# Mixer C of a two-layer encoder: 32 by 32 diagonal blocks gathered by copies of ScalarE instead of masks and sums of VectorE

## The chip, the cores and the metric

The kernel runs on one core of a Trainium2 chip. The metric is the device time of one execution in microseconds (us), the median of the runs shown. The engines are TensorE (PE in the profile; its weight loads are PEld), VectorE (DVE), ScalarE (ACT), GpSimd (POOL) and the queue of SyncE (SP), which issues nearly all transfers. Each engine executes its own instructions in order; semaphores let one wait for another.

## The reference, cut to what matters

The reference is an encoder of two layers over 256 tokens of 1024 channels. In each layer four mixers work on one joint projection of x: A (a gated mLSTM), B (dilated attention), C (a gated delta rule) and D (windowed attention). Their outputs are gated, summed and projected, and a feed-forward part follows: a SwiGLU in layer 0, eight experts in layer 1. Mixer C has 4 heads of 64 channels and runs in two directions over chunks of 64 tokens. For each chunk, head and direction it solves a triangular system of 64 unknowns:

```python
a_strict = jnp.where(strict, jnp.einsum('bhnid,bhnjd->bhnij', k_beta, k) * decay, 0.0)
rhs = jnp.concatenate([v * beta[..., None], k_beta * jnp.exp(gc)[..., None]], axis=-1)
sol = lax.linalg.triangular_solve(a_strict, rhs, left_side=True, lower=True, unit_diagonal=True)
u, w = sol[..., :Dv], sol[..., Dv:]
```

The rest of the mixer is a scan over the chunks with matrix products.

## The kernel before, in words

**The large products.** The weights are 32-bit. Each piece of 128 by 1024 is loaded into `raw` (line 251), ScalarE rounds it into a high half `wh` (line 256), and VectorE, sometimes GpSimd, subtracts to get the low half `wl` (line 259). TensorE multiplies three times (line 162): high by high, high by low, low by high. So each group of products needs one cast of ScalarE and one subtraction of VectorE first. `raw`, `wh` and `wl` live in rings of a few buffers: a cast waits until TensorE has finished with the buffer that it is to write.

**The mixers** are Python generators. `mixing` (line 1151) issues the projections one after the other and after each piece advances the open mixers by some steps, so that their small instructions stand between the large products. The order on each engine is made by a planner when the kernel is built: it takes instructions by priority as their inputs come ready in its own model of time, and a mixer's steps get a priority that is raised by 56 places (`AHEAD`). After that the order is fixed: an instruction that waits holds up all behind it on its engine.

**Mixer C** (`mix_c`, line 745). `systems(t)` makes, for each half t of the tokens (128 each) and direction d, a tile U of 128 partitions by 4 heads by 128 columns, which holds the triangular systems. `leaves(d)` (line 869) inverts the 32 by 32 blocks on U's diagonal, four for each head and half, all at once; `unit(d, t)` (line 911) combines the inverses with TensorE into the full ones (V is the transpose of W, the two tiles of the inverse) and advances the scan.

`leaves` first has to bring the blocks together. The diagonal blocks lie at partitions 32k to 32k+31 and columns 32k to 32k+31 of each head. Line 879 multiplies U by the mask `blk32`, in which partition group k is one for block k only, into a tile `cum`; line 880 sums over k, so that each partition keeps the 32 columns of its own block, and writes them into y at a distance of 32 elements. Line 882 copies the result three more times, and line 883 transposes all 32 by 32 blocks of y into z. Then come 31 steps of forward substitution on VectorE (lines 897 and 898, two instructions of 0.2 to 0.3 us each) that update `cX`, a transpose into `cWc` (line 902), and for each half t line 906 spreads the result back: a product with the same mask writes W, zero outside the diagonal blocks, and line 907 transposes it into V.

After that `unit(d, d)` runs first, then `unit(d, 1 - d)`. In `unit`, the first product (line 924) reads U and W, the second (line 931) reads V. The next direction's solve starts when the first one's `cWc` is written, because `cX` has one buffer. `cW` and `cV` have two buffers each, and `cum` shares a ring of two (`cs`) with the tiles of `systems`. `leaves` runs four times in all, twice a layer.

Of the kernel before, what the change touches and what calls it, by code (L numbers as in the profile page):

```python
# [12 lines left out]
OP = mybir.AluOpType  # L13
AX = mybir.AxisListType
PSUM = bass.MemoryType.PSUM

P = 128
# [102 lines left out]
class Encoder:  # L120
# [624 lines left out]
    def mix_c(self):  # L745
        mp, nc, c = self.mp, self.nc, self.c
# [89 lines left out]
        r3 = lambda x: x[:].rearrange("p (h i) -> p h i", i=P)  # L836
        U, at, V, W = {}, {}, {}, {}
# [31 lines left out]
        def leaves(d):  # L869


            yz = self.m8("cYZ")
            y, z = yz[:, :1024], yz[:, 1024:]
            yv = y.rearrange("p (i x t h) -> p i x t h", x=4, t=2, h=4)
            k32 = c["blk32"][:, None, :, None].to_broadcast([P, 4, 4, 32])
            for t in range(2):
                m = self.t2("cum", "cs")
                mv = m[:].rearrange("p (h k i) -> p h k i", k=4, i=32)
                self.tt(mv, U[d, t].rearrange("p h (k i) -> p h k i", i=32), k32, OP.mult)
                nc.vector.tensor_reduce(yv[:, :, 0, t, :].rearrange("p i h -> p h i"), mv.rearrange("p h k i -> p h i k"), AX.X, OP.add)  # L880
            y4 = y.rearrange("p (i x m) -> p i x m", x=4, m=8)
            nc.vector.tensor_copy(y4[:, :, 1:4], y4[:, :, 0:1].to_broadcast([P, 32, 3, 8]))
            nc.vector.transpose(z, y)
            zv = z.rearrange("p (i j) -> p i j", j=32)
            x = mp.tile([P, 8, 32], F32, name="cX", bufs=1)
            nc.gpsimd.tensor_copy(x[:], c["own32b"].rearrange("p (q r) -> p q r", q=8))
            tmp = mp.tile([P, 8, 32], F32, name="cXt", bufs=1)
            yield
            for n in range(31):
                i = 31 - n if d else n  # L890
                rows = slice(0, i) if d else slice(i + 1, 32)
                cs = slice(i // 4, 8) if d else slice(0, i // 4 + 1)
                sh = [P, cs.stop - cs.start, rows.stop - rows.start]
                f = zv[:, rows, i][:, None].to_broadcast(sh)
                pv = x[:, cs, i:i + 1].to_broadcast(sh)
                tv = tmp[:, cs, rows]
                self.tt(tv, f, pv, OP.mult)
                self.tt(x[:, cs, rows], x[:, cs, rows], tv, OP.subtract)
                if n % 3 == 2:
                    yield  # L900
            wc = mp.tile([P, 256], F32, name="cWc", bufs=1)
            nc.vector.transpose(wc[:], x[:].rearrange("p q r -> p (q r)"))
            wcv = wc[:].rearrange("p (c t h) -> p t h c", t=2, h=4)
            for t in range(2):
                w, vv = self.t2("cW", "cW"), self.t2("cV", "cV")
                self.tt(w[:].rearrange("p (h k c) -> p h k c", k=4, c=32), wcv[:, t][:, :, None, :].to_broadcast([P, 4, 4, 32]), k32, OP.mult)
                nc.vector.transpose(vv[:], w[:])
                W[d, t], V[d, t] = r3(w), r3(vv)
            yield
# [86 lines left out]
        for d in range(2):  # L996
            yield from leaves(d)
            both = [unit(d, t) for t in (d, 1 - d)]
            for _ in range(3):
                for q in both:  # L1000
                    next(q)
                    yield
# [636 lines left out]
```

## Time and profile before

| what | value |
|---|---|
| median of 3 runs | 1399.38 us (1396.96 to 1399.58) |
| the profiled execution, its own time | 1402.63 us |
| its span, first to last instruction | 1400.8 us |
| granted TensorE clock, mean over the span | 0.979 of full speed |
| TensorE busy | 1331.2 us (95%) |
| VectorE busy | 1074.6 us (77%) |
| ScalarE busy | 744.2 us (53%) |
| GpSimd busy | 146.2 us (10%) |

Busy is the time in which an engine executes instructions; matmuls are pipelined and their ends are modelled, so a busy TensorE is not one at its peak. The page also cuts the span into 40 slices of 35 us. `leaves` runs in slices 3 to 6 (layer 0, about 102 to 190 us) and 20 to 22 (layer 1, about 680 to 766 us):

```profile
PE   7999999999999999999989999997999999999995
DVE  6879876775885655678888478568988888888887
ACT  5535453454364443344434446434777778677673
PEclk9999999999999999999999999998999999999997
```

Each digit is the busy share of one slice in tenths (9 is 90% or more), counted from slice 0 at the left. PEclk is the clock granted to TensorE in tenths of full speed.

### The profile page before, as it was taken

Reading aid. Unit: us, or ns where it says so; the run is one execution under the profiler, and the core shown is the slowest. Engines: PE = TensorE matmul, PEld = TensorE weight load, DVE = VectorE, ACT = ScalarE, POOL = GpSimd, SP = SyncE. Lnnn points to the kernel's source line nnn. Section 1 sums busy time; section 2 is a strip of 40 time slices with the busy share of each in tenths; the row PEclk is TensorE's granted clock in tenths of the full one; section 3 lists DMA queues with packets and bytes.
Section 4 is the critical chain, followed back from the end, with each engine's and each line's share of the span. In section 5 each row is a group of like instructions: output and inputs, shape, how many; then the busy total and the mean of one; then the engine's idle time right before and its main releaser. Section 6 shows DMA issues by size and latency. Waiting matters only on the chain. (4 is left out here: it accounts for less than half of the span.)

```text
span 1400.8 us, 23007 instructions
## 1 busy us (share of the span) xinstructions
PE 1331.2 (95%) x8699; PEld 1151.7 (82%) x8702; DVE 1074.6 (77%) x1869; ACT 744.2 (53%) x1097; POOL 146.2 (10%) x119
## 2 busy tenths in 40 slices
PE   7999999999999999999989999997999999999995
PEld 7877879989889998888678889986778878877873
DVE  6879876775885655678888478568988888888887
ACT  5535453454364443344434446434777778677673
POOL 1000200022200000100120001220211110211110
PEclk9999999999999999999999999998999999999997
DMA  7532512485596553234152237745989899989982
GB/s 248 172 106 65 157 61 77 151 304 183 174 299 185 193 187 100 96 103 127 59 161 91 76 104 266 245 127 184 350 301 377 307 328 325 359 309 353 354 307 76
DMA packets 155750, 281.90 MB, mean 201 GB/s; under 512 B 11120, under 2 KB 58480, under 8 KB 155632
## 3 DMA queue, kind: packets, MB, share of 16 engines
q1 hardware_dynamic: 153136, 273.54, 57.9%
q10 hardware_dynamic: 1152, 4.19, 0.9%
q0 software_dynamic: 1344, 2.62, 0.5%
q8 instruction: 70, 1.15, 0.3%
q14 instruction: 48, 0.39, 0.1%
HBM read 276.65 MB, written 2.10 MB: 199 GB/s over the span
## 5 line engine op out<-in xcount | busy, mean ns | idle before, releaser
L259 DVE TENSOR_TENSOR wl<-raw,wh 128x1024 fp32r<-128x1024 f32 (+3 forms) x515 | 612.9, 1217 | 155.3 <-ACT wh L256 139.9
L256 ACT CAST wh<-raw 128x1024 fp32r<-128x1024 f32 (+3 forms) x539 | 525.1, 1006 | 311.5 <-PE mm L162 244.3
L162 PE MATMUL mm<-wh,xh 128*128 128x512 f32 (+4 forms) x736 | 192.0, 370 | 3.8 <-ACT wh L256 2.5
L162 PE MATMUL mm<-wh,xl 128*128 128x512 f32 (+4 forms) x736 | 184.3, 365 | 0.0
L162 PE MATMUL mm<-wl,xh 128*128 128x512 f32 (+4 forms) x544 | 149.9, 368 | 8.5 <-DVE wl L259 8.5
L162 PE MATMUL mm<-xh,wh 128*128 128x256 f32 x960 | 142.3, 287 | 13.2 <-ACT wh L256 7.3
L162 PEld LDWEIGHTS mm<-wh,xh 128*128 128x128 f32 x736 | 129.8, 190 | 26.9 <-ACT wh L256 4.8
L162 PEld LDWEIGHTS mm<-wh,xl 128*128 128x128 f32 x736 | 130.7, 190 | 19.9 <-issue 0.7
L162 PE MATMUL mm<-xl,wh 128*128 128x256 f32 x960 | 141.2, 287 | 0.0
L162 PE MATMUL mm<-xh,wl 128*128 128x256 f32 x960 | 138.2, 282 | 0.0
L162 PEld LDWEIGHTS mm<-xh,wh 128*128 128x128 f32 x960 | 125.4, 192 | 15.5 <-ACT wh L256 7.3
L162 PEld LDWEIGHTS mm<-xl,wh 128*128 128x128 f32 x960 | 126.0, 193 | 1.1 <-issue 0.3
L162 PEld LDWEIGHTS mm<-xh,wl 128*128 128x128 f32 x960 | 123.2, 189 | 0.8 <-issue 0.2
L162 PEld LDWEIGHTS mm<-wl,xh 128*128 128x128 f32 x544 | 94.7, 191 | 25.8 <-DVE wl L259 10.8
L259 POOL TENSOR_TENSOR wl<-raw,wh 128x1024 fp32r<-128x1024 f32 (+1 forms) x24 | 62.0, 2585 | 343.5 <-ACT wh L256 250.9
L1056 POOL TENSOR_TENSOR mg<-mg,th 128x512 f32<-128x512 f32 x24 | 44.5, 1883 | 360.2 <-DVE th L142 360.2
L162 PE MATMUL mm<-wh,hth 128*128 128x512 f32 x176 | 56.6, 397 | 0.0
L162 PE MATMUL mm<-wl,xl 128*128 128x512 f32 (+1 forms) x192 | 56.6, 376 | 0.0
L162 PE MATMUL mm<-wl,hth 128*128 128x512 f32 x176 | 55.7, 395 | 0.0
L162 PE MATMUL mm<-wh,htl 128*128 128x512 f32 x176 | 55.6, 394 | 0.0
L162 PE MATMUL mm<-yT,wh 128*128 128x256 f32 x320 | 43.2, 284 | 0.0
L162 PEld LDWEIGHTS mm<-wl,xl 128*128 128x128 f32 x192 | 35.7, 188 | 6.1 <-DVE wl L259 0.5
(371 smaller groups left out, 1713.9 us busy)
## 6 DMA issues: line engine op xcount, KB each, us to landing
raw<-moe_w_in SPq DMA_DIRECT2D x215, 512.0 KB, 6.2
raw<-w_in_in SPq DMA_DIRECT2D x132, 512.0 KB, 4.1
raw<-ffn_w_in SPq DMA_DIRECT2D x66, 512.0 KB, 3.7
raw<-moe_w_in SPq DMA_DIRECT2D x64, 384.0 KB, 4.5
raw<-w_out_in SPq DMA_DIRECT2D x16, 512.0 KB, 3.5
raw<-w_branch_d_in SPq DMA_DIRECT2D x8, 512.0 KB, 4.8
raw<-w_in_in SPq DMA_DIRECT2D x8, 396.0 KB, 3.6
raw<-w_branch_b_in SPq DMA_DIRECT2D x4, 512.0 KB, 3.3
```

The costliest lines, as they stand in the source:

```text
L162: return self.nc.tensor.matmul(o, l, r, start=start, stop=stop, skip_group_check=True)
L256: self.nc.scalar.copy(h[:, :m * n], raw[:, :m * n])
L259: eng.tensor_sub(l[:, :m * n], raw[:, :m * n], h[:, :m * n])
L1056: self.nc.gpsimd.tensor_tensor(m, m, x, OP.add)
```

## The change

Line 879 and 880 (masks and sums) become eight copies of ScalarE in each `leaves`: for each half t and each block k, the 32 partitions of the block by 4 heads by 32 columns go from U straight to their place in y. The copy that repeats the result three times moves from VectorE to ScalarE. At the end, line 906 (the product with the mask) becomes a memset of W by GpSimd and four copies of ScalarE, one for each block. The transposes stay on VectorE. The tile `cum` is no longer used, and the last loop takes the halves in the order d, 1 - d instead of 0, 1.

```diff
-            k32 = c["blk32"][:, None, :, None].to_broadcast([P, 4, 4, 32])
+            parts = [slice(32 * k, 32 * k + 32) for k in range(4)]
             for t in range(2):
-                m = self.t2("cum", "cs")
-                mv = m[:].rearrange("p (h k i) -> p h k i", k=4, i=32)
-                self.tt(mv, U[d, t].rearrange("p h (k i) -> p h k i", i=32), k32, OP.mult)
-                nc.vector.tensor_reduce(yv[:, :, 0, t, :].rearrange("p i h -> p h i"), mv.rearrange("p h k i -> p h i k"), AX.X, OP.add)
+                for r in parts:
+                    nc.scalar.copy(yv[r, :, 0, t, :].rearrange("p i h -> p h i"), U[d, t][r, :, r])
             y4 = y.rearrange("p (i x m) -> p i x m", x=4, m=8)
-            nc.vector.tensor_copy(y4[:, :, 1:4], y4[:, :, 0:1].to_broadcast([P, 32, 3, 8]))
+            nc.scalar.copy(y4[:, :, 1:4], y4[:, :, 0:1].to_broadcast([P, 32, 3, 8]))
             nc.vector.transpose(z, y)
...
-            for t in range(2):
+            for t in (d, 1 - d):
                 w, vv = self.t2("cW", "cW"), self.t2("cV", "cV")
-                self.tt(w[:].rearrange("p (h k c) -> p h k c", k=4, c=32), wcv[:, t][:, :, None, :].to_broadcast([P, 4, 4, 32]), k32, OP.mult)
+                nc.gpsimd.memset(w[:], 0.0)
+                for r in parts:
+                    nc.scalar.copy(r3(w)[r, :, r], wcv[r, t])
                 nc.vector.transpose(vv[:], w[:])
                 W[d, t], V[d, t] = r3(w), r3(vv)
```

## Rows read from the trace of the kernel before

**Rows 1.** The page's busy times: us (share of the span) xinstructions, whole span.

```profile
PE 1331.2 (95%) x8699; PEld 1151.7 (82%) x8702; DVE 1074.6 (77%) x1869; ACT 744.2 (53%) x1097; POOL 146.2 (10%) x119
```

**Rows 2.** Waits of PE, 684:730 and 148:153: us in total, times, longest us.

```profile
PE mm L162 <- DVE wl L259: 3.7, 1, 3.7
...
PE mx L162 <- DVE cW L134: 1.2, 1, 1.2
```

**Rows 3.** Timeline 723:726: start us, us, engine, line, op, out<-in, xcount [idle before <-releaser].

```profile
723.47 0.45 DVE L902 STREAM_TRANSPOSE cWc<-cX 128x256 f32<-128x256 f32 x1
...
724.15 2.21 DVE L134 TENSOR_TENSOR cW<-cWc,c 128x512 f32<-128x512 f32 x2
...
725.40 0.46 PE L162 MATMUL mx<-cW,cU 32*32 32x32 f32 x16 [1.88 <-DVE cW L134]
```

**Rows 4.** Tile view of cW, under "who waited for it (us, times)".

```profile
  PE mx L162: 3.6, 3
```

**Rows 5.** Timeline of PE, 697:708.

```profile
697.79 0.64 PE L162 MATMUL mm<-wh,xl 128*128 128x256 f32 x4
702.15 1.22 PE L162 MATMUL mm<-wl,xh 128*128 128x512 f32 x4 [3.72 <-DVE wl L259]
```

**Rows 6.** Timeline of ACT, 685:800.

```profile
693.72 1.05 ACT L256 CAST wh<-raw 128x1024 fp32r<-128x1024 f32 x1 [1.20 <-PE mm L162]
...
697.87 0.79 ACT L145 ACTIVATE bk<-mx 128x128 f32<-128x128 f32 x4 [2.43 <-PE mx L166]
707.26 0.59 ACT L508 COPY bvn<-mm 128x512 f32<-128x512 f32 x1 [8.60 <-PE mm L162]
```

**Rows 7.** Timeline of DVE, 680:702.

```profile
680.56 1.12 DVE L142 SCALAR_TENSOR_TENSOR cU<-mx,cbeta,cdec 128x128 f32<-128x128 f32 x4 [1.31 <-ACT cdec L145]
...
693.71 0.68 DVE L134 TENSOR_TENSOR cum<-cU,c 128x512 f32<-128x512 f32 x1
...
695.27 1.10 DVE L880 TENSOR_REDUCE cYZ<-cum 128x128 f32<-128x512 f32 x1
...
699.63 1.23 DVE L883 STREAM_TRANSPOSE cYZ<-cYZ 128x1024 f32<-128x1024 f32 x1
...
700.88 1.21 DVE L259 TENSOR_TENSOR wl<-raw,wh 128x1024 fp32r<-128x1024 f32 x1
```

**Rows 8.** Groups by form, DVE, whole span: xcount | busy us, mean ns | idle before.

```profile
L134 DVE TENSOR_TENSOR cW<-cWc,c 128x512 f32<-128x512 f32 x8 | 8.8, 1139 | 0.1
L880 DVE TENSOR_REDUCE cYZ<-cum 128x128 f32<-128x512 f32 x8 | 8.6, 1075 | 0.0
L134 DVE TENSOR_TENSOR cum<-cU,c 128x512 f32<-128x512 f32 x8 | 5.5, 684 | 0.0
...
L882 DVE COPY cYZ<-cYZ 128x768 f32<-128x768 f32 x4 | 2.2, 552 | 0.0
```

**Rows 9.** Windows: stretch, us, busy us of each engine, PEclk (granted clock), DMA share, GB/s.

```profile
703.00:707.00 4.00, 4.00 (x12) 3.14 (x11) 3.73 (x12) 0.00 (x0) 0.00 (x0) 0.57 0.88 253
727.00:731.00 4.00, 4.00 (x49) 3.71 (x48) 3.65 (x9) 2.62 (x4) 2.04 (x4) 0.57 0.41 129
148.00:152.00 4.00, 2.66 (x32) 2.40 (x33) 3.79 (x10) 1.53 (x5) 2.55 (x4) 1.00 0.73 218
```

**Rows 10.** Groups by form, ACT, whole span.

```profile
L256 ACT CAST wh<-raw 128x768 fp32r<-128x768 f32 x64 | 51.1, 838 | 10.7 <-PE mm L162 10.6
...
L208 ACT CAST yT<-yb 128x256 fp32r<-128x256 f32 x4 | 2.6, 653 | 0.7 <-DVE yb L134 0.7
...
L208 ACT CAST ath<-mm 128x256 fp32r<-128x256 f32 x4 | 1.5, 376 | 0.0
```

**Rows 11.** Groups by form, POOL, whole span.

```profile
L834 POOL MEMSET cS<- 128x256 f32 x4 | 1.2, 323 | 0.0
```

**Rows 12.** Waits of all engines, whole span: us in total, times, longest us.

```profile
ACT wh L256 <- PE mm L162: 244.3, 215, 3.1
```

## The prediction

> **What bounds the kernel now.** I read the page first: TensorE is busy 95% of the span and ScalarE 53% [rows 1], so a change on VectorE and ScalarE can win only what TensorE loses while it waits for them, and only in the two stretches where mixer C runs. I went on from the page to the waits of TensorE in those stretches, to the timeline of each engine around the longest wait, and to the granted clock there.
>
> In layer 1, between 684 and 730 us, TensorE waits 3.7 us once for a low weight half `wl` [rows 2] and 1.9 us once for `cW` [rows 3]. The tile view of `cW` puts all of TensorE's waits for it at 3.6 us in three places [rows 4]: these 1.9, then 1.2 at 150 us in layer 0 [rows 2], and so 0.5 at the third, in layer 1's second direction at 766 us.
>
> The wait for `wl` is the one to look at closely. TensorE ends a group at 698.4 and starts the next at 702.15 [rows 5]. ScalarE had the high half `wh` done at 694.8 [rows 6]; VectorE turned to `wl` only at 700.88 [rows 7]. From 693.71 until then its queue held, among other things, the whole preparation of the second direction of `leaves`: two masks, two sums, the copy and the transpose. In front of this `wl` stand 0.68 + 1.10 + 0.69 + 1.05 + 0.55 = 4.1 us of the very instructions that the change takes from VectorE ([rows 7] show the first of the two pairs, whose second ran at 697.16 and 697.92; the copy's 0.55 is in [rows 8]).
>
> [...] I call 3.7 + 1.7 = 5.4 us gap 1, and 1.9 + 1.7 = 3.6 us gap 2.
>
> **The change part by part.** *Off VectorE.* 8 masks (5.5 us), 8 sums (8.6), 4 copies (2.2) and 8 products into `cW` (8.8) go: 25.1 us in four calls [rows 8], 6.3 a call. The two transposes of the blocks stay. Nearly all of this lies beside TensorE's work; on the path lie the 4.1 us in front of the `wl` of gap 1. With them gone and nothing put in their place, that `wl` starts near 696.8 and is ready at 698.0, before TensorE asks at 698.4. I count gap 1 as gone: -5.4 us. Late next on VectorE would be the solve's steps and the `wl`s behind this one, each of 1.2 us.
>
> *Onto ScalarE.* 64 copies of 32 partitions by 128 elements and 4 copies of 128x768. No row shows a copy of this shape with both operands in SBUF. Below stands the dense one of 128x128 from PSUM, four in 0.79 us [rows 6], 0.20 each: 12.6 us for 64. Above stands a strided one: the split of `yb` into `yT`, which writes every fourth element, takes 0.653 us for 256 elements where a dense one takes 0.376 [rows 10]; 0.277 more for 256 is 0.14 for 128, so 0.34 each and 21.8 us. The 128x768 copy goes by the cast of that shape, 0.84 [rows 10], 3.4 for four. Together 16 to 25 us; I take the strided end, as both copies gather elements that lie apart (512 bytes in U, 32 bytes in `wcv`). [...]
>
> ScalarE is idle from 698.7 to 707.26 in the place of gap 1 [rows 6], and over the run its extra 25 us raise it from 744 to 769 us. The block copies need only U, whose last part was done at 681.7 [rows 7]; so most of them fill its idle time, and I cost them at nothing. Without that cover the price is a `wh` cast that comes up to 2.7 + 0.84 = 3.5 us late behind one call's block copies.
>
> *The wait that is added, at the blocks.* The transpose of the blocks on VectorE now waits for 9 instructions of ScalarE. Behind it in VectorE's order stand solve steps and `wl`s, and for those TensorE waits. At gap 1 that decides: 0 if ScalarE ran the copies in its earlier idle time, all of gap 1 back if they stand behind the `bk` copies, which themselves waited for TensorE until 697.87 [rows 6]: 698.7 + 2.7 + 0.8 + 1.23 (transpose) + 1.21 (`wl`) = 704.6 against 702.1 now. I take 0, because nothing of higher priority needs ScalarE for that long before 697.
>
> *The wait that is added, at W.* TensorE's first product of a unit needs W of the first t. Before: the transpose `cWc` ends at 723.92, `cW` follows, and TensorE starts at 725.40 [rows 3], 1.5 us later. After: four copies by 0.34, 1.36 us, and two hand-overs between engines, for which I add 0.1 each (an estimate from 0.15 us between the end of the first `cW` and TensorE's start): 1.6. By the dense price it would be 1.0. In layer 1 the path stays the same within 0.1. In layer 0, where no `wl` stands between, the 1.14 us of one `cW` [rows 8] and a hand-over, 1.25, become 1.6: +0.3. In the second direction the first unit is t = 1, whose W was the second product and now comes first, 1.1 us sooner: the 0.5 us wait goes. The order of t costs nothing else. ScalarE's queue is held meanwhile, and behind it stand `wh` casts, which are made ahead of use.
>
> *GpSimd.* 8 memsets of 128x512; the one of 128x256 takes 0.32 us [rows 11], so 0.32 to 0.65 each. They need only a free `cW` buffer, which in the first direction is free from the start and in the second from the end of the first direction's solve, a whole solve ahead. I cost them at nothing; a `bv` transfer in front of one in GpSimd's order would be the price, and by 0.65 us for each.
>
> *The sum.* -5.4 (gap 1) + 0.1 (gap 2) + 0.3 (layer 0) - 0.5 (second direction) = -5.5 us against the profiled execution, 1402.6, which makes 1397.1. That execution lay 3.2 us above the median of the three runs, 1399.4; against the median it is 1393.9, say **1394.0**. Its own range, with gap 1 between half and wholly gone and gap 2 shorter by half at best, is 1391 to 1397.
>
> **The rivals.** *All of the gaps close* (-5.4 - 3.6 - 1.2 - 0.5 = -10.7): 1388.7. For it: 8 us of what goes (the block preparation of both calls) stand ahead of the first `cW` of a layer on the same engine. Against it: the order of TensorE is planned with the shorter work too, and its place for W moves up as well.
>
> *The wait only changes its name.* VectorE stands at the transpose of the blocks, waiting for ScalarE, and gap 1 stays (704.6 against 702.1 worked out above, at worst), or the new order, planned anew for every engine, opens another gap of that size: 1399.4, give or take 2. For it: the copies are the lowest in priority when they are issued. Against it: ScalarE's idle time.
>
> *Slower: W behind a held cast.* ScalarE takes its instructions in order. If a `wh` cast stands in front of the W copies, they start late by its wait for TensorE, 244.3 us over 215 waits or 1.1 us on average [rows 12], and its own 1.05: 2.2 us in each of the four places, where TensorE has just shown that it waits for W. In layer 0 the two waits then pass 1.9 us, where the clock fell, 1.7 each: 4 x 2.2 + 2 x 1.7 - 5.4 = +6.8, 1406.2. It decides from 5.4 / 4 = 1.35 us of lateness per place. For it: three of four places already wait for W. Against it: over the run ScalarE is idle 47% of the time [rows 1], and if a cast is held for TensorE, TensorE still has matmuls of its own to run.
>
> **How the numbers follow.** About 0.2% (2.8 us) is what a measurement of this kernel can tell from no change. The forecast 0.45, all gaps closed 0.13, the wait under another name 0.23, slower 0.19. Faster by over 0.2% takes the first two less the part of the first above 1396.6, 0.55; within it, 0.26; slower, 0.19. The range runs from 1388 (all gaps) to 1403 (half of the slower case).
>
> **What would show it.** Right: no wait of TensorE for `wl` over 2 us between 684 and 730 us and a granted clock of 1.00 behind the place; VectorE busy some 25 us less than before, ScalarE near 769 us; 0.3 us or more for a block copy; the waits for `cW` now for ScalarE, still about 1 to 2 us. Wrong: the transpose of `cYZ` with an idle time before it that ScalarE ended; W copies that start more than 1.4 us after `cWc`; new waits of TensorE for `wh` in 90 to 150 or 684 to 770 us; the clock falling at a place where it had held.

## The result, and the profile after

The changed kernel is slower: 1411.34 us median of 20 runs (1399.41 to 1422.79), against 1397.59 for the kernel before in the same job (20 runs, 1393.36 to 1400.47). The ratio is 1.0095, with a 95% interval of 1.0073 to 1.0116. The forecast was 1394.0 us. Ratios and their intervals, here and below, leave out executions more than 1.5% above the fastest of their kernel (2 of these 20, the tail of the loss described below), while medians, clocks and net times are of all executions.

The profiled execution took 1399.5 us, which is the short end of those runs; another profiled execution (e1, below) took 1405.1. The page's busy times, in us, answer to [rows 1]:

```profile
PE 1335.7 (96%) x8699; PEld 1156.4 (83%) x8702; DVE 1055.5 (76%) x1841; ACT 773.6 (55%) x1165; POOL 151.1 (11%) x127
```

The waits of all engines over the span (us in total, times, longest us) answer to [rows 2] and [rows 4]:

```profile
PE mm L162 <- DVE wl L259: 4.8, 5, 1.0
...
PE mx L162 <- ACT cW L906: 2.8, 2, 2.0
...
DVE cYZ L881 <- ACT cYZ L880: 1.1, 1, 1.1
```

The 3.7 us wait for `wl` is gone: none is longer than 1.0. TensorE's waits for `cW` are 2.8 us in all where they were 3.6, the longest 2.0 where it was 1.9. TensorE's idle time, the span less its busy time on the page, fell from 69.6 to 61.9 us. By the waits alone the forecast stands. What does not stand is the clock. The timeline at W in layer 1, the place of [rows 3]:

```profile
711.70 0.44 DVE L900 STREAM_TRANSPOSE cWc<-cX 128x256 f32<-128x256 f32 x1
712.18 3.51 ACT L906 COPY cW<-cWc 32x128 f32<-32x128 f32 x8 [2.06 <-DVE cWc L900]
...
712.65 0.43 PE L162 MATMUL mx<-cW,cU 32*32 32x32 f32 x8 [1.99 <-ACT cW L906]
...
713.97 0.63 PE L162 MATMUL mx<-cW,cU 32*32 32x32 f32 x8
...
715.71 0.85 ACT L256 CAST wh<-raw 128x792 fp32r<-128x792 f32 x1
```

and the windows around it (columns as in [rows 9]; the last three are the granted clock, the DMA share and GB/s):

```profile
698.00:703.00 5.00, 5.00 (x45) 5.00 (x44) 4.62 (x17) 1.56 (x3) 2.17 (x4) 1.00 0.59 163
708.00:713.00 5.00, 2.71 (x24) 2.11 (x22) 3.86 (x15) 2.29 (x8) 1.32 (x3) 1.00 0.42 118
713.00:718.00 5.00, 5.00 (x56) 4.39 (x54) 3.07 (x8) 3.42 (x8) 2.20 (x5) 0.50 0.40 125
723.00:728.00 5.00, 5.00 (x30) 3.90 (x29) 0.52 (x3) 1.21 (x4) 0.79 (x2) 0.50 0.89 321
733.00:738.00 5.00, 5.00 (x29) 4.76 (x29) 1.92 (x9) 2.51 (x6) 0.00 (x0) 0.50 0.00 0
738.00:743.00 5.00, 5.00 (x36) 5.00 (x35) 4.21 (x12) 1.71 (x3) 0.00 (x0) 0.77 0.05 7
743.00:748.00 5.00, 5.00 (x45) 4.41 (x44) 4.05 (x12) 1.19 (x3) 0.00 (x0) 1.00 0.80 216
```

TensorE waits 1.99 us for W, as it waited 1.88 before. Behind that wait the clock lay at 0.50 of full speed from 713 to about 740 us, where before it was back at 1.00 by 731:

```profile
731.00:734.00 3.00, 3.00 (x38) 2.40 (x37) 2.10 (x8) 0.47 (x2) 0.00 (x0) 1.00 0.48 161
```

(this row is of the kernel before). In those 27 us TensorE is recorded as busy all the time, with 29 or 30 products in 5 us (723 and 733 us) against 45 at the full clock (698 and 743 us); VectorE, which waits 8.08 us for one of its products (until 731.67), is busy 0.52 of 5 us in 723 to 728. By the clock, 27 us at 0.50 lose 13.5, an estimate.

The 20 runs show the same as a sum. Their time follows the mean clock of the execution: 1399.5 us at 0.975, 1411 at 0.968, 1419 at 0.960. If an execution of 1400 us loses 1400 x (1 - clock), what is left is an estimate of its time at full clock, called *net* here: 1372 us before and 1364 after. So the changed kernel has 8 us less to do on the path, and pays for it with a mean clock of 0.967 instead of 0.982, 21 us. (Among the 20 runs themselves 0.01 of the clock goes with 12.8 us, where the estimate takes 14; by that slope it is some 5 us less to do and 19 us paid.)

The prices of the new instructions, groups by form of ScalarE and of GpSimd (xcount | busy us, mean ns | idle before):

```profile
L906 ACT COPY cW<-cWc 32x128 f32<-32x128 f32 x32 | 13.7, 429 | 6.5 <-DVE cWc L900 6.0
L878 ACT COPY cYZ<-cU 32x128 f32<-32x128 f32 x32 | 13.3, 416 | 1.2 <-DVE cU L142 0.9
L880 ACT COPY cYZ<-cYZ 128x768 f32<-128x768 f32 x4 | 3.3, 833 | 0.1
```

```profile
L904 POOL MEMSET cW<- 128x512 f32 x8 | 4.1, 528 | 4.7 <-DVE cV L907 2.8 <-PE mx L162 1.8
```

### The profile page after: what moved, and what is told of

It reads as the page before. It is cut to its first block, busy times and chain, and to the rows that moved or that the text cites. A ratio compares the mean times of both kernels' runs of the same rounds, so it can differ in the third digit from the quotient of the medians.

```text
span 1397.6 us, 23081 instructions
## 1 busy us (share of the span) xinstructions
PE 1335.7 (96%) x8699; PEld 1156.4 (83%) x8702; DVE 1055.5 (76%) x1841; ACT 773.6 (55%) x1165; POOL 151.1 (11%) x127
## 5 line engine op out<-in xcount | busy, mean ns | idle before, releaser
L162 PE MATMUL mm<-wh,xl 128*128 128x512 f32 (+4 forms) x736 | 187.5, 369 | 0.0
L162 PE MATMUL mm<-wl,xh 128*128 128x512 f32 (+4 forms) x544 | 153.5, 372 | 4.8 <-DVE wl L259 4.8
L162 PE MATMUL mm<-xh,wh 128*128 128x256 f32 x960 | 139.4, 285 | 9.3 <-ACT wh L256 6.6
L162 PE MATMUL mm<-xl,wh 128*128 128x256 f32 x960 | 138.0, 283 | 0.0
L162 PEld LDWEIGHTS mm<-xl,wh 128*128 128x128 f32 x960 | 123.2, 189 | 1.0 <-issue 0.5
```

The costliest lines, as they stand in the source:

```text
L162: return self.nc.tensor.matmul(o, l, r, start=start, stop=stop, skip_group_check=True)
```

## The experiments

Two theories were set against each other. *Clock*: the loss is TensorE's clock, which falls behind a wait and stays down because few large products stand beside the small ones of the units. *Queue*: ScalarE's copies hold the casts behind them, TensorE waits, and the clock only follows. In the expectations, theory 1 and the theory of the mix are *clock*, theory 2 and the theory of ScalarE are *queue*; those of e2 and e3 say which half of the change each would blame. "Large products" are those of the projections (`mm`, 128x256 to 128x264); they are counted below in TensorE's instruction order from the first product that reads W to the last product of that unit, in the first direction of layer 0 / layer 1. That order is fixed when the kernel is built. The table has all kernels but e1, e5 and e8 (in the text below), each with 6 to 20 executions; "mean clock" is the median over them of the granted clock of a whole execution, and the ratio is to the kernel before in the same job:

| kernel | large products | mean clock | median us | ratio (95%) |
|---|---|---|---|---|
| before (all jobs) | 42/44 | 0.982 | 1396.3 to 1397.7 | 1 |
| the change | 35/35 | 0.967 | 1411.3 | 1.0095 (1.0073 to 1.0116) |
| e2 blocks only | 43/42 | 0.982 | 1392.2 | 0.9962 (0.9938 to 0.9987) |
| e3 W only | 35/43 | 0.976 | 1404.8 | 1.0058 (1.0025 to 1.0092) |
| e4 order of t only | 42/44 | 0.982 | 1396.7 | 1.0011 (0.9990 to 1.0033) |
| e6 W copies on VectorE | 37/45 | 0.979 | 1397.4 | 0.9995 (0.9949 to 1.0041) |
| e7 wider steps | 37/37 | 0.974 | 1399.4 | 0.9996 (0.9956 to 1.0035) |
| e9 fill ahead of W | 35/38 | 0.974 | 1405.1 | 1.0037 (1.0005 to 1.0068) |
| e10 blocks only, fill | 43/38 | 0.981 | 1395.4 | 0.9984 (0.9962 to 1.0006) |
| e11 other order of blocks | 33/39 | 0.967 | 1411.4 | 1.0086 (1.0051 to 1.0121) |
| e12 blocks only, idle copies | 34/42 | 0.973 | 1405.9 | 1.0031 (1.0002 to 1.0059) |
| e13 W of t = 1 later, 300 | 52/62 | 0.976 | 1399.6 | 1.0009 (0.9989 to 1.0029) |
| e14 W of t = 1 later, 250 | 52/34 | 0.974 | 1404.0 | 1.0045 (1.0024 to 1.0065) |
| e15 W copies on GpSimd | 34/41 | 0.974 | 1409.0 | 1.0092 (1.0065 to 1.0119) |
| e16 blocks only, later W | 61/63 | 0.984 | 1386.3 | 0.9930 (0.9905 to 0.9956) |
| e17 before, later W, 300 | 68/45 | 0.983 | 1396.5 | 0.9991 (0.9967 to 1.0015) |
| e18 before, later W, 150 | 34/45 | 0.982 | 1395.6 | 1.0011 (0.9991 to 1.0031) |

**The parts one by one.** e1 is the change once more. e2 has the block copies, with W by the mask on VectorE and the halves in the order 0, 1 (the edit at W):

```diff
-                nc.gpsimd.memset(w[:], 0.0)
-                for r in parts:
-                    nc.scalar.copy(r3(w)[r, :, r], wcv[r, t])
+                self.tt(w[:].rearrange("p (h k c) -> p h k c", k=4, c=32), wcv[:, t][:, :, None, :].to_broadcast([P, 4, 4, 32]), k32, OP.mult)
```

e3 has the new W with the blocks as before, and e4 only the order of t:

```diff
-            for t in range(2):
+            for t in (d, 1 - d):
```

> The changed kernel as it is, for a profile of an ordinary execution (its profiled one was among its shortest, 1399.5 us at a mean granted clock of 0.975; most lay at 1409 to 1420 and 0.968 to 0.96). Theory 1 (clock): TensorE does the same work and waits no longer than in the short execution, and the 10 to 20 us more are stretches of 20 us or more at the lower clock behind the first direction's wait for W, in layer 0, in layer 1 or in both; time and mean clock go together, some 14 us for 0.01. Theory 2 (queue): ScalarE's copies hold up casts, and TensorE's waits for wh or wl add up to 10 us more than before, with the clock a consequence.

> Only the blocks by ScalarE; W by the masked product of VectorE as before, halves in the order 0, 1. Theory 1: what moves the units among other large products is the shorter work of VectorE before the solve, so this kernel has the long stretch at the lower clock too: 1405 to 1415, clock under 0.97. Theory 2 (the W copies do the harm): 1391 to 1396, as the gain without the harm.

> Only W by a memset and ScalarE's copies; blocks by masks and sums as before, halves in the order 0, 1. Theory 1: near the kernel before, 1395 to 1401, clock 0.975 or more, as the solve ends where it did. Theory 2: 1405 to 1415, with the wait for W at 2 us or more in each layer.

> The kernel before with the halves of the last loop in the order d, 1 - d, nothing else. Both theories: within 2 us of before; the wait for W in the second direction of layer 1 (0.5 us) gone. If this one is slower by 5 us or more, the order of t moved the units and neither theory's reason is the cause.

e1 took 1405.1 us at a clock of 0.972, with 0.50 from about 717 to 741 us: the stretch is no accident of one profile. e2 is faster than both kernels, e3 slower, e4 neither. So the block copies give what was forecast for the change, -5.3 us (-8.7 to -1.8), and the harm comes with W. In e3 TensorE waits for W 0.65 us in layer 0 and 1.03 us in layer 1, less than in the kernel before, and the kernel is slower all the same. The parts do not add up: 0.4% won, 0.6% and 0.1% lost make 0.3%, and the change loses 0.95%. Each variant is planned anew, and e3's order in layer 1 keeps 43 large products where the change's has 35. e2's windows at W in layer 1, behind a wait of 2.07 us:

```profile
710.00:715.00 5.00, 2.93 (x35) 2.68 (x35) 4.79 (x12) 1.00 (x3) 3.31 (x5) 0.95 0.67 212
715.00:720.00 5.00, 5.00 (x69) 4.29 (x67) 3.83 (x13) 1.62 (x3) 2.09 (x4) 0.70 0.38 113
720.00:725.00 5.00, 5.00 (x46) 4.03 (x45) 2.65 (x11) 2.38 (x8) 0.04 (x1) 1.00 0.70 222
```

The wait is as long as the changed kernel's, but the clock is back at 1.00 by 720. What differs is TensorE's order behind the wait, here with the number of products of each kind:

```
changed: W 4, large 3, W 4, large 6,  V 5, W 8, V 3, large 5, V 8, large 2, transposes 4, large 6
e2:      W 8, large 15,               V 5, W 8, V 3, large 9, V 8, large 1, transposes 4, large 4
```

**Large products added, small pieces moved.** e5 and e8 put a dense product without use in front of each group of the first direction's units, in the changed kernel and in the kernel before; e6 makes the W copies on VectorE; e7 gives each step of those units one more place in the turn of the mixers:

```diff
+            def bank():
+                o = self.bmx()
+                if d == 0:
+                    self.mm(o[:], c["identb"], c["mbb"][:, :512])
+                return o
...
-                    nc.scalar.copy(r3(w)[r, :, r], wcv[r, t])
+                    nc.vector.tensor_copy(r3(w)[r, :, r], wcv[r, t])
...
                     next(q)
                     yield
+                    if d == 0:
+                        yield
```

> The changed kernel with a dense product of 128x512 more in front of each group of small products in the units of the first direction (some 40 in all, about 9 us of TensorE at full clock; what they write is overwritten). Theory 1 (TensorE's clock stays low because too few large products stand beside the units): the clock comes back soon after the wait for W, 0.98 on average, and the kernel with more work is faster than the changed one: 1393 to 1402. Theory 2 (ScalarE's W copies hold up other work, the clock only follows): the added work is paid in full, 1415 to 1425, clock 0.96 to 0.97.

> The changed kernel with the eight small copies into W on VectorE instead of ScalarE; memset, shape and order as in the change. If the small pieces let the units start while few large products are ready (theory 1, by granularity): clock under 0.975 and 1405 to 1415, as in the changed kernel. If ScalarE's 3.5 us for eight copies put the casts, and so the large products, behind (theory 1, by the casts, or theory 2): 1390 to 1396 and 0.98, as with the masked product.

> The changed kernel with one more place given up to the projections after each step of the first direction's units, so that more large products are issued between them. Theory 1: the stretch at the lower clock is 3 to 10 us and no longer 25, 1390 to 1400. Theory 2: no change from the changed kernel, 1405 to 1415.

> The kernel before with the same dense products added: the price of them where the clock is not low. Both theories: 3 to 10 us slower than before, clock 0.98 or more. If it is faster than before, the clock costs that kernel something in its units too.

e5 took 1410.2 us (four executions; ratio 1.0119, 1.0068 to 1.0170) and e8 1407.9 (seven; 1.0083, 1.0053 to 1.0112). The fillers cost some 10 us of net time in both. In the kernel before they left the clock alone (0.981), in the changed kernel they raised it from 0.967 to 0.975, which gives back about what they cost. In e5's profile the stretch at 0.50 behind W in layer 1 is 7 us long (716 to 723 us). That bears the clock theory out in sign and falls short of its figure. e6 falls into two groups of runs, six from 1388 to 1398 us at a clock of 0.979 to 0.986 and four from 1408 to 1416 at 0.965 to 0.971; e7 spreads from 1385 us (0.986) to 1409 (0.967). The same program can fall or not, and that VectorE makes the small pieces does not take the second group away.

**Filling the wait.** e9 and e10 (the change, and e2) send nine products into the place where TensorE waits for W in layer 1:

```diff
+            if d == 0 and self.layer:
+                o = self.bmx()
+                self.mm(o[:, :8], c["ident"], x[:, :, 29])
+                for _ in range(8):
+                    self.mm(o[:], c["identb"], c["mbb"][:, :512])
             wc = mp.tile([P, 256], F32, name="cWc", bufs=1)
```

> The changed kernel, with a chain of nine products without use (one of 128x8 that reads a finished row of cX, then eight bf16 products of 128x512) on TensorE just ahead of the first product that reads W, in layer 1's first direction only: it stands where TensorE waits 2 us for W, starts when the solve's third step from the end is done, and so should fill that wait and cost some tenths of a us. Clock theory (the 2 us of idleness and the thin work behind them start the stretch at the lower clock): no stretch at 0.50 from 713 to 740 us, mean clock 0.975 to 0.985, and 1393 to 1402 us. Queue theory (ScalarE's W copies hold the casts, the clock only follows): no difference from the changed kernel, 1407 to 1412 us, low stretch as before.

> Block copies on ScalarE, W by the product with the mask as in the kernel before, and the same nine products ahead of the first product that reads W in layer 1. Both theories agree on the blocks. Clock theory: the 3.4 us stretch at a lower clock behind the wait for W goes too, 1.7 us: 1389 to 1392 us. Queue theory: nothing is won, 1392 to 1394 us.

The fill missed its place, as e10's timeline of TensorE shows; so neither run tests what filling the wait is worth:

```profile
713.88 0.36 PE L162 MATMUL mx<-cX,c 128*128 128x8 f32 x2 [2.25 <-DVE cX L134]
714.32 3.17 PE L162 MATMUL mx<-c 128*128 128x512 bf16 x7
717.41 0.57 PE L162 MATMUL mx<-cW,cU 32*32 32x32 f32 x16
```

The 2.25 us of idleness stand in front of the fill instead of behind it, and W's products come 3 us late; e10 took 1395.4 us, more than either theory gave it. What the fill became is a dense run behind a wait. In e9 the wait is 2.34 us, until 732.20, and the clock of layer 1 lies at 0.50 for 3.4 us only, where the change's lay there for 27:

```profile
730.00:735.00 5.00, 2.57 (x8) 1.18 (x10) 3.86 (x17) 2.17 (x6) 1.36 (x3) 0.74 0.37 108
735.00:740.00 5.00, 5.00 (x71) 3.79 (x69) 3.43 (x10) 3.77 (x11) 2.36 (x6) 0.92 0.14 34
```

e9 differs from the change in layer 1 alone and took 1389 us at 0.983 in its best run, 1411 at 0.969 in others. Its profiled execution is its longest, 1415.8 us, and lost its clock in layer 0, where its order and its waits are the change's: 0.50 for 24 us from 142 and for 27 us from 196 us. In the change's own profile those places show no fall and one of 3.4 us.

**ScalarE or the order.** e11 takes the four W copies in another order, e12 leaves W on VectorE and lets ScalarE make the 32 copies all the same, into a tile that is not read:

```diff
-                for r in parts:
+                for r in parts[1 - d::2] + parts[d::2]:
                     nc.scalar.copy(r3(w)[r, :, r], wcv[r, t])
...
+                extra = mp.tile([P, 4, 32], F32, name="cextra", bufs=2)
+                for r in parts:
+                    nc.scalar.copy(extra[r], wcv[r, t])
```

> The changed kernel, with the four W copies of each half in another order, so that both blocks which the first products of the unit read come last: the same work for ScalarE in the same place, but TensorE gets its 16 first products closer together and 13 instead of 6 or 7 large products stand between the first W products and the first V products. Clock theory, if what stands in the units decides: nearer to the kernel with W by the mask, 1395 to 1403 us, clock 0.975 or more. Queue theory: 1408 to 1413 us, as the changed kernel, and 0.4 us more for the first product.

> Block copies on ScalarE, W by the product with the mask on VectorE, and beside it the 32 small W copies of ScalarE all the same, into a tile that nobody reads: 32 x 0.42 = 13.5 us more for ScalarE in the same places, with TensorE's order nearly that of the kernel without them. Queue theory: the casts behind them come late and the loss is there, 1400 to 1412 us. Clock theory: TensorE does not wait for these copies, 1391 to 1396 us, clock 0.98 or more.

e12 answers the queue theory's figure, but by the clock: its net time is e2's, 1365.9 against 1366.2 us, and its clock 0.973 against 0.982. I had written that its order was nearly e2's; counted, it is not so in layer 0. There TensorE waits 1.24 us for W in e2 and 1.21 in e12, and behind it stand 15 large products before the next small group in e2 and 10 in e12, 43 and 34 up to the unit's end, which I put down to casts that the plan sets behind the extra copies (not shown). Windows of layer 0, first e2:

```profile
138.00:143.00 5.00, 3.69 (x50) 3.25 (x51) 4.80 (x10) 1.34 (x2) 3.33 (x5) 1.00 0.40 130
143.00:148.00 5.00, 5.00 (x74) 4.20 (x72) 4.67 (x15) 2.21 (x5) 0.00 (x0) 1.00 0.19 43
148.00:153.00 5.00, 5.00 (x46) 4.22 (x46) 2.03 (x10) 1.49 (x5) 2.13 (x4) 1.00 0.37 123
```

then e12:

```profile
138.00:143.00 5.00, 3.57 (x65) 3.02 (x65) 4.81 (x9) 4.42 (x10) 1.38 (x2) 1.00 0.19 65
143.00:148.00 5.00, 5.00 (x44) 4.00 (x42) 3.04 (x10) 2.30 (x5) 2.00 (x4) 0.69 0.33 99
148.00:153.00 5.00, 5.00 (x29) 4.00 (x29) 1.68 (x5) 1.63 (x5) 0.07 (x1) 0.50 0.28 89
```

The clock is back at 1.00 by 162. In layer 1, where e12's order has e2's 15 and 42, its clock falls for a few us only (0.70 in 730 to 735, 0.96 after). The second direction of layer 0 adds a second ingredient. There TensorE's order is the same in e2, e12, e15 and the change, but its wait in front of W's products differs. In the first three it is for `bp`, an instruction of another mixer on ScalarE, which itself stood idle for VectorE's `bnm` (3.32, 2.54 and 5.18 us), so that it is VectorE's work which comes later; in e15 VectorE had waited 1.11 and 1.22 us for GpSimd's copies of W. The timelines of e2, e12, e15 and the change, in that order:

```profile
184.29 0.33 PE L166 MATMUL mx<-c,bp 128*128 128x128 f32 x1 [1.18 <-ACT bp L145]
```

```profile
191.40 0.33 PE L166 MATMUL mx<-c,bp 128*128 128x128 f32 x1 [1.42 <-ACT bp L145]
```

```profile
186.02 0.33 PE L166 MATMUL mx<-c,bp 128*128 128x128 f32 x1 [3.10 <-ACT bp L145]
```

```profile
184.73 0.33 PE L166 MATMUL mx<-c,bp 128*128 128x128 f32 x1 [1.77 <-DVE ale L142]
```

Behind it the clock held in e2, and lay at 0.50 in e12 from about 193 to 216 us and in e15 from about 187 to 211. In the change it fell behind the longer wait, 1.77 us, for 3.4 us only, where e12's fell behind 1.42 us for 24. Windows of the change, then of e12:

```profile
185.00:190.00 5.00, 5.00 (x52) 4.19 (x51) 1.95 (x9) 2.59 (x5) 0.00 (x0) 0.73 0.08 31
190.00:195.00 5.00, 5.00 (x64) 3.75 (x63) 2.53 (x5) 0.39 (x2) 0.00 (x0) 0.92 0.17 37
```

```profile
195.00:200.00 5.00, 5.00 (x39) 4.05 (x39) 2.00 (x8) 1.63 (x2) 0.00 (x0) 0.50 0.00 0
```

So with one order of TensorE behind it, the length of the wait does not give the length of the stretch. e11 moved the wrong way: 33/39, with 9 and 8 large products ahead of the first V product where 13 were expected, and 1411.4 us.

**The order changed, the copies kept, and the other way round.** In e13 and e14, W of the second half of the first direction gets a priority 300 or 250 places lower, so that more casts and large products go ahead of it; e15 has the W copies on GpSimd; e16 is e2 with the 300 places; e17 and e18 are the kernel before with 300 and 150:

```diff
             for t in (d, 1 - d):
+                late = 300 if d == 0 and t == 1 else 0
+                self.tc.cur_priority += late
                 w, vv = self.t2("cW", "cW"), self.t2("cV", "cV")
...
                 W[d, t], V[d, t] = r3(w), r3(vv)
+                self.tc.cur_priority -= late
```

> The changed kernel, all its copies on ScalarE; W of the second half (t = 1) of the first direction is issued with a priority 300 places lower, so that casts and large products go ahead of it: 52 and 62 large products (layer 0, layer 1) instead of 35 and 35 stand on TensorE between the first product that reads W and the last of the first unit. Theory of the mix (few large products beside the units let the clock fall and stay down): no stretch at 0.50 longer than 6 us in 135 to 170 and 705 to 750 us, mean clock 0.980 or more, 1386 to 1394 us. Theory of ScalarE (its 32 W copies do it, wherever the products stand): 1402 to 1412 us.

> The same with 250 places instead of 300: 52 large products beside the first unit in layer 0, but 34 in layer 1. Theory of the mix: layer 1's stretch at the lower clock stays (20 us or more from about 715), layer 0 keeps its clock; mean clock 0.972 to 0.978, 1394 to 1404 us, between the changed kernel and the one with 300. Theory of ScalarE: like the one with 300, whatever that is.

> The changed kernel, with the 32 W copies on GpSimd instead of ScalarE: ScalarE is as free as with blocks only, but TensorE's order has 34 and 41 large products beside the first unit. Theory of the mix: layer 0's clock falls for some 18 us in many of the executions, mean clock 0.970 to 0.977, 1396 to 1408 us. Theory of ScalarE: clock 0.98 or more, 1388 to 1395 us, and some us more if GpSimd's copies are slow.

> Block copies on ScalarE, W by the product with the mask on VectorE, and W of the second half of the first direction issued 300 places lower: 61 and 63 large products beside the first unit instead of 43 and 42. Theory of the mix: clock 0.983 or more, 1385 to 1392 us, as fast as blocks only or some us faster. Theory of ScalarE: as blocks only, 1391 to 1394 us.

> The kernel before, none of the change in it; only W of the second half of the first direction is issued 300 places lower in priority: 68 and 45 large products beside the first unit instead of 42 and 44. Theory of the mix: clock 0.983 or more, 1392 to 1396 us; the wait for wl in layer 1 (3.7 us) stays, so it cannot reach the 1386 us of the kernel that has the block copies as well. If the gain of 6 us over blocks only came from W's place itself, 1390 us or less.

> The same with 150 places: 34 and 45 large products beside the first unit. No instruction is added to or taken from any engine; only the order differs. Theory of the mix: layer 0's clock falls for some 18 us in many of the executions, mean clock 0.970 to 0.978, 1398 to 1408 us, slower than before. If instead the copies' time on an engine is what costs the clock: 1396 to 1398 us, as before.

e13 and e14 have the same instructions on every engine as the change, and the same 2.0 us wait for W in layer 1. The two orders of TensorE are alike up to 3 us behind that wait, and in both the clock falls within 1 us of its end. Windows of e13 (62 large products there), then of e14 (34):

```profile
715.00:720.00 5.00, 2.73 (x25) 2.12 (x23) 3.81 (x15) 2.33 (x9) 1.38 (x3) 1.00 0.41 120
720.00:725.00 5.00, 5.00 (x53) 4.19 (x52) 2.87 (x7) 3.27 (x7) 1.63 (x4) 0.55 0.52 161
725.00:730.00 5.00, 5.00 (x45) 4.68 (x45) 3.67 (x10) 1.99 (x4) 2.48 (x5) 0.77 0.55 183
730.00:735.00 5.00, 5.00 (x47) 4.30 (x47) 4.14 (x14) 3.63 (x7) 0.21 (x1) 1.00 0.53 161
```

```profile
710.00:715.00 5.00, 3.11 (x25) 2.62 (x25) 3.01 (x12) 3.41 (x9) 2.46 (x5) 0.76 0.59 181
715.00:720.00 5.00, 5.00 (x62) 4.14 (x62) 3.41 (x10) 2.49 (x5) 0.52 (x1) 0.50 0.00 0
725.00:730.00 5.00, 5.00 (x26) 4.18 (x25) 0.00 (x0) 0.74 (x2) 0.00 (x0) 0.50 0.29 108
735.00:740.00 5.00, 5.00 (x38) 4.91 (x37) 2.84 (x9) 2.64 (x4) 0.00 (x0) 0.85 0.01 2
```

The clock falls in both; with 62 large products it is back within 10 us, with 34 it stays down for over 20. All profiles of layer 1 agree with that, one execution each: the clock lies at 0.50 behind W for 24 to 27 us in the five with 34 to 39 large products and no fill (the change, e1, e7, e11, e14), and for 7 us at most in the eleven with 41 or more and in the four with a fill (e5, e8, e9, e10).

Against the kernel before, the change loses 0.95%, e14 0.45% and e13 0.1%, and their net times lie within 3 us of each other (1364, 1367, 1366). So the same instructions in another order give the loss back, and they do it by the clock. Two things limit this. The later W also shortens the wait in front of W's products in the second direction of layer 0, 1.77 us in the change and 0.49 and 0.53 here, so that the large products beside the first unit are not all that changed. And e13 lies 4.4 us below e14 in the same job, but their mean clocks, 0.976 and 0.974, are closer than 12 executions of each can tell apart; of the two profiled executions e14's has the higher (0.975 against 0.973), as e13's clock fell at more places elsewhere. e13 missed the 1386 to 1394 us expected: its clock still falls behind W, for some 7 us a layer; between W and the next small group 9 large products stand, as in the change. e15 takes the W copies off ScalarE and stays slow, at 0.974; its net time is 1371.7, 5.5 us over e2's, so that a third of what it loses to e2 is not clock. A copy costs about as much there:

```profile
L906 POOL COPY cW<-cWc 32x128 f32<-32x128 f32 x32 | 14.2, 444 | 48.2 <-DVE cWc L900 31.9 <-DVE af L605 14.8
```

So ScalarE's busy time as such is not the cause. e16 is the fastest kernel of all, 1386.3 us, 0.7% below the kernel before; its interval overlaps e2's, so that a gain over e2 is not shown, and its net time is e2's within 1.2 us. e17 shows that the later W is worth nothing in the kernel before (68/45, and no gain; I had expected up to 4 us); the product of e2's and e17's ratios, 0.9953, lies inside e16's interval, so that the two need not add more together than alone.

e18 sets a limit to this account, and missed the 1398 to 1408 us expected. It has 34 large products beside the first unit of layer 0, no copy on ScalarE, a wait of 1.26 us, and loses nothing:

```profile
148.00:153.00 5.00, 4.03 (x77) 3.57 (x78) 4.57 (x11) 1.73 (x3) 3.07 (x6) 1.00 0.36 120
153.00:158.00 5.00, 5.00 (x56) 3.98 (x53) 3.98 (x12) 1.52 (x5) 1.30 (x3) 1.00 0.44 140
```

The count is therefore no law. Shown is that the change's loss is clock and not waits (net times, and TensorE's idle time), and that with the same instructions on every engine another order takes nearly all of it away (the change against e13, ratios 1.0073 to 1.0116 and 0.9989 to 1.0029). In layer 1 the length of the stretch went with TensorE's order behind W in every profile. Not shown is that the order alone decides: in layer 0 the change's order lost nothing in one execution and 24 us at 0.50 in another (e9's). Open is which property of the order and of the wait in front makes the clock fall, and why the same program falls in some executions only.

## Why the prediction was wrong

*Gap 1* was right in place and size. The 1.7 us that both gaps hold for the clock is no measured time: the trace of the kernel before shows 3.4 us at 0.50 behind each of the two waits (the 0.57 of [rows 9]), and by that clock this makes 1.7. -5.4 us were forecast for gap 1; e2, which holds nothing else of weight, measures -5.3 (-8.7 to -1.8), and no wait for `wl` over 1.0 us is left in it or in the change. One sign of it missed: VectorE's busy time fell by 19.1 us, where 25 were forecast.

*ScalarE's copies at nothing* held for the block copies (e2 has them, at the clock of the kernel before) and not for W's. The price was too low for both: a copy takes 0.42 to 0.43 us, over the 0.34 of the upper bound, so 30 us in all (page: +29.4) instead of 25. They are hidden in the sense in which I used the word: TensorE waits no longer than before. But the cover was counted in ScalarE's idle time only, and not in what the planner does with TensorE's order. Beside the first units that order has 35 and 35 large products with W by small copies, and 43 and 42 with W by the mask. Casts that come later behind the copies may be one way to this (e12 has 34 in layer 0); they are not the only one, as W by GpSimd's copies gives 34 and 41 (e15).

*The wait added at the blocks*: 0 forecast; VectorE's transpose waits once, 1.1 us, and TensorE's waits show nothing of it. This was one of the listed signs of being wrong, and it came.

*The wait added at W* is the step that failed. I priced the arrival of W: +0.1 us in layer 1, which came (1.88 to 1.99); +0.3 in layer 0, where the wait became 0.4 shorter (1.23 to 0.85); -0.5 in the second direction, where it went. What stands behind the copies I put at nothing, with the words that the `wh` casts "are made ahead of use", and the sum kept the 1.7 us of gap 2 for the clock as if a fall of it had a fixed price. The runs showed that price to change with TensorE's order behind the wait: 1.7 us in the kernel before, 13.5 in the profile after, 3.4 in e13 (7 us at 0.50). Over all executions and places the mean clock puts the loss at some 20 us, four times the gain.

*The rivals.* The slower one, "W behind a held cast", lies near in time (1406.2) and is wrong in mechanism: ScalarE began W 0.04 us after `cWc` was done (0.04 to 0.09 in three of the four places), and it is the cast that stood behind W (715.71 us above), not W behind a cast. In the fourth place, the second direction of layer 0, W did begin 2.08 us after `cWc`, behind casts and other mixers' copies, another of the listed signs; but TensorE came to W 11 us after `cWc` and did not wait for it. The sign nearest to the loss was the last in my list, the clock falling at a place where it had held. In layer 1 the clock had fallen before too, and now it stayed down; in layer 0 it fell where it had held, in e1's profile for 3.4 us:

```profile
140.00:145.00 5.00, 5.00 (x67) 4.32 (x66) 3.24 (x9) 3.14 (x6) 2.87 (x6) 0.66 0.12 43
```

That sign had a line there and no term in the sum: I had the 1.00 of [rows 9] in layer 0 beside the 0.57 in layer 1, and did not ask why the clock fell behind one wait and not behind another. (The row that I read for layer 0, 148 to 152 us, lies mostly ahead of the end of that wait at 151.1; in the next window of the kernel before, 152 to 156, the clock is 1.00 too.)

*The range* of 1388 to 1403 ended 8 us below the median. A bound was missing: a clock at 0.50 through the units of one direction, 27 us in the profile after, costs some 13 by the estimate above.

## What to carry to other kernels

Price a change near a stretch with small products on TensorE also by what TensorE does just behind its waits, and not by the length of the waits alone: here 2.0 us of waiting went with 7 us at a clock of 0.50 in e13 and with 24 in e14. Where a planner fixes the order, instructions that add no wait can still move large products away (42 and 44 became 35 and 35 here); compare TensorE's order before and after, and the mean granted clock of many executions, before looking for waits. When a part of a change pays and another harms, run the parts: here the half that leaves W alone, with W of the second half issued later, gives 1386.3 us, where the half alone gave 1392.2 (their intervals overlap).

## What the runs showed of the hardware

The granted clock stayed at 0.50 of full speed for 27 us while TensorE was recorded as 100% busy, with small products between 35 large ones (the change, layer 1). Behind waits of 2.0 us with the same instructions on every engine it stayed there for 7 us in one order of TensorE and for 24 in another (e13, e14). With one and the same order it stayed for 3.4 us behind a wait of 1.77 us and for 24 behind 1.42 (the change and e12, second direction of layer 0). The mean clock differed between executions of one program (e6: six runs at 0.979 to 0.986, four at 0.965 to 0.971), and with it the time, 1388 to 1416 us. A copy of 32 partitions by 128 elements into W, which reads every eighth element and writes runs of 32, takes 0.43 us on ScalarE (the change), 0.44 on GpSimd (e15) and 0.29 on VectorE (e6).
